# Column sums of the modulation vectors: one-column matmuls replaced by two wide matmuls and diagonal sums on VectorE

## The chip, the core and the metric

The kernel runs on one core of a Trainium2 chip. The number that counts is the device time of one execution in microseconds (us); where a time is given for a kernel it is the median of its runs. The engines are TensorE (PE; PEld is its weight load), VectorE (DVE), ScalarE (ACT), GpSimd (POOL) and SyncE (SP), which here issues the DMAs. TensorE writes to PSUM, and the other memory on the chip is SBUF.

## The reference, cut to what matters

Four layers work on x of shape (1024, 1024). Layer i uses mixer i mod 3: gated linear attention (GLA), spatial gating (SGU), forgetting attention (FoX), then GLA again. Each layer is modulated by a vector that depends only on the small input c:

```python
cond = jax.nn.silu(c)
for i in range(DEPTH):
    mod = (cond @ w_mod[i] + b_mod[i])[:, None, :]
    shift, scale, gate = jnp.split(mod, 3, axis=-1)
    h = rms_norm(x, norm_pre_g[i]) * (1.0 + scale) + shift
    ...  # the mixer turns h into o
    x = x + gate * rms_norm(o, norm_post_g[i])
```

The change concerns how `shift` and `scale` of layers 1, 2 and 3 are brought into the form in which they are used.

## The kernel before

All of the input and output projections run on TensorE in three passes (lines 357 to 359): a weight and an activation are each split into a rounded part (float32r, the type of the fast multiplication, names `whi`, `wo`, `hTh`) and the rest (`wlo`, `hTl`), and three of the four products are summed in a PSUM tile `pj`. There are three PSUM tiles for the projections (tag `pj`), three for small work (`pm`) and two for scores (`pb`).

The modulation is 3072 numbers a layer, in six pieces of 512 (`j` = 0 to 5 in `mod_pieces`). For a piece, an accumulator `acc` of 128 x 512 (a tile of tag `md`, of which there are four) starts as zero with the bias in row 0. For each of eight blocks of 128 rows of `w_mod`, VectorE adds the block times a column of `cond` (L264). The piece is then the sum of `acc` over its 128 partitions, and `finish` takes this sum:

- Pieces 4 and 5 (the gate) are wanted as rows, the same in each partition. ScalarE rounds `acc` to `hi` (L289), GpSimd takes the rest `lo` (L290), and TensorE multiplies both with a square of ones (`onesr`, L291 and L292).
- Pieces 0 to 3 (shift and scale) are wanted as columns, the feature in the partition, as `SH` and `G` of 128 x 8. TensorE takes each 128 x 128 block of `acc` as the weights against one column of ones (L274), four matmuls with one output column each. These are full float32, and each is two matmul records in the trace. VectorE copies the four columns to `SH` (L278) or combines them into `G` (L281).

Layer 0 takes its pieces in a wide form at the start (`wide=True`, PSUM tile `pb`). For the later layers the pieces are background work: while layer l runs, the pieces 0 to 3 of layer l+1 are worked on, one step of a piece at a time, so that 12 of these `finish` calls fall into layers 0, 1 and 2, four in each (names in the trace: `pm<-ones,md`).

The order in which each engine does its instructions is not the order of the Python text. The compiler front end that builds the program orders the instructions of each engine by a simulated timeline, and each engine then does its own list strictly in order. Work tiles of tag `s2` (shown as `s`) come from a pool of 28.

In the GLA layer `mix` builds 7 levels of decayed products on VectorE and ScalarE (lines 702 to 712), whose scores TensorE takes (L723) and VectorE merges into `cmix` (L725); a running state `st` is updated at L778. In the FoX layer `weigh` takes scores (L1119, L1120), and VectorE adds a bias and takes the maximum in one instruction with an accumulator (L1123, L1128, shown as a custom operation and the read of its accumulator); `do_v` brings projections from `pj` to `v` (L1025 on ScalarE, L1026 on VectorE).

Of the kernel before, what the change touches and what calls it, by code (L numbers as in the profile page):

```python
# [8 lines left out]
F32 = mybir.dt.float32  # L9
F32R = mybir.dt.float32r  # L10
U8 = mybir.dt.uint8
AF = mybir.ActivationFunctionType
ALU = mybir.AluOpType
AX = mybir.AxisListType

P = 128
# [78 lines left out]
class Trunk:  # L95
# [124 lines left out]
        nc.gpsimd.memset(self.cmix, 0.0)  # L220


    def mod_pieces(self, l, cols, wide=False):
        nc, a = self.nc, self.a
        if cols[0] < 4 and self.G[l] is None:
            self.G[l] = self.cp.tile([P, KT], F32, name=f"G{l}")
            self.SH[l] = self.cp.tile([P, KT], F32, name=f"SH{l}")
        if cols[-1] >= 4:
            self.gg[l] = self.cp.tile([P, D], F32, tag="gg", name=f"gg{l}", bufs=2)
        G, SH, gg = self.G[l], self.SH[l], self.gg[l]  # L230
        pieces, ends = [], []

        def col(j):
            st = {}

            def begin():
                acc = self.sp.tile([P, 512], F32, tag="md", name=self.nm("md"), bufs=4)
                nc.gpsimd.memset(acc, 0.0)
                nc.sync.dma_start(out=acc[0:1, :], in_=a["b_mod"][l:l + 1, j * 512:(j + 1) * 512])
                st["acc"] = acc  # L240
                if wide:
                    st["pt"] = self.ps("pb")
                    nc.tensor.matmul(st["pt"][:, 0:4], self.ident, self.zero, start=True, stop=False)

            def step(kp):
                w = []
                if wide:
                    wt = self.wp.tile([P, 2, 512], F32, tag="whl", name=self.nm("md2"))
                    self.last["sp"] = nc.sync.dma_start(out=wt, in_=a["w_mod"][l, 2 * kp * P:(2 * kp + 2) * P, j * 512:(j + 1) * 512]
                                      .rearrange("(i p) n -> p i n", p=P))  # L250
                    w = [wt[:, i, :] for i in range(2)]
                else:
                    for i in range(2):
                        w.append(self.sp.tile([P, 512], F32, tag="md", name=self.nm("md"), bufs=4))
                for i in range(2):
                    kt = 2 * kp + i
                    if wide and kp % 2 and i:
                        for c in range(4):
                            nc.tensor.matmul(st["pt"][:, c:c + 1], w[i][:, c * P:(c + 1) * P], self.cond[:, kt:kt + 1],
                                             start=False, stop=False)  # L260
                        continue
                    if not wide:
                        nc.sync.dma_start(out=w[i], in_=a["w_mod"][l, kt * P:(kt + 1) * P, j * 512:(j + 1) * 512])
                    ins = nc.vector.scalar_tensor_tensor(st["acc"], w[i], self.cond[:, kt:kt + 1], st["acc"],  # L264
                                                         op0=ALU.mult, op1=ALU.add)
                    if not wide:
                        self.tc.keep_in_program_order(ins)

            def finish():
                acc = st["acc"]  # L270
                if j < 4:
                    pt = st["pt"] if wide else self.ps("pm")
                    for i in range(4):
                        self.last["tensor"] = nc.tensor.matmul(pt[:, i:i + 1], acc[:, i * P:(i + 1) * P], self.ones[:, 0:1],  # L274
                                                               start=not wide, stop=not wide or i == 3)
                    k0 = (j % 2) * 4
                    if j < 2:
                        nc.vector.tensor_copy(SH[:, k0:k0 + 4], pt[:, 0:4])  # L278
                    else:
                        g0 = self.vcol["gpre"] + l * KT + k0  # L280
                        nc.vector.scalar_tensor_tensor(G[:, k0:k0 + 4], pt[:, 0:4], 1.0, self.vec[:, g0:g0 + 4],  # L281
                                                       op0=ALU.add, op1=ALU.mult)
                else:
                    cs = (j - 4) * 512
                    gp = self.s2([512])
                    nc.sync.dma_start(out=gp, in_=a["norm_post_g"][l:l + 1, cs:cs + 512].partition_broadcast(P))
                    pt = self.ps("pm")
                    hi, lo = self.s2([512], F32R), self.s2([512], F32R)
                    nc.scalar.copy(hi, acc)  # L289
                    nc.gpsimd.tensor_tensor(lo, acc, hi.bitcast(F32), op=ALU.subtract)  # L290
                    nc.tensor.matmul(pt, self.onesr, hi, start=True, stop=False)  # L291
                    nc.tensor.matmul(pt, self.onesr, lo, start=False, stop=True)  # L292
                    nc.vector.tensor_tensor(gg[:, cs:cs + 512], pt, gp, op=ALU.mult)

            pieces.append(lambda: (begin(), step(0)))
            if ends:
                pieces.append(ends.pop())
            for kp in range(1, 4):
                pieces.append((lambda kp: lambda: step(kp))(kp))
            ends.append(finish)  # L300
            if wide or j == cols[-1]:
                pieces.append(ends.pop())

        for j in cols:
            col(j)
        return pieces
# [1026 lines left out]
```

## Time and profile before

| | |
|---|---|
| runs | 2140.03, 2142.40, 2142.49 us; median 2142.4 us |
| profiled execution | 2135.41 us |
| its span from first to last instruction | 2133.7 us |
| TensorE clock granted, mean | 0.994 |
| TensorE busy | 2070.1 us, 97% of the span |
| VectorE busy | 1304.2 us, 61% |
| ScalarE busy | 906.4 us, 42% |
| GpSimd busy | 802.2 us, 38% |

Outside its span the profiled execution has 1.7 us, and it took 7.0 us less than the median of the runs. Layer 0 runs to about 560 us, layer 1 to about 850 us, layer 2 to about 1600 us, and the rest is layer 3. A matmul's duration in the trace overlaps the next one's, so what a matmul costs is read from one start to the next.

### The profile page before, as it was taken

What the parts mean: (1) busy time and instruction counts of PE and PEld (TensorE: products, weight loads), DVE (VectorE), ACT (ScalarE), POOL (GpSimd) and SP (SyncE); (2) the same over time, 40 slices, a digit from 0 to 9 for tenths busy, and PEclk for the clock granted to TensorE, in tenths of its full rate; (3) what the DMA queues carried; (4) which work ended last, traced back from release to release, by engine and by line L of the source; (5) the groups of instructions that cost most, each with busy time, mean ns of one, the idle gap of its engine ahead of it and who ended that gap; (6) DMA issues with size and microseconds to landing.
All of it is one profiled execution on the core that took longest, in us unless ns stands there. A gap on an engine that the chain in (4) does not pass through costs nothing. (4 is left out here: it accounts for less than half of the span.)

```text
span 2133.7 us, 35726 instructions
## 1 busy us (share of the span) xinstructions
PE 2070.1 (97%) x13637; PEld 1848.4 (87%) x13637; DVE 1304.2 (61%) x2884; ACT 906.4 (42%) x1905; POOL 802.2 (38%) x735
## 2 busy tenths in 40 slices
PE   6999999999999999999999999999999999999998
PEld 6888998988998888898788898898678899899987
DVE  7686878645465425556656656656865654776642
ACT  4555333335322114544445445445545655343331
POOL 5433333355343332535333333333323441342351
PEclk9999999999999999999999999999999999999999
DMA  8132222424425432423223323323424320112322
GB/s 295 41 90 79 84 81 96 149 99 138 138 76 164 132 117 99 136 71 104 81 75 100 90 70 101 88 71 100 148 81 143 101 60 21 50 46 69 127 90 95
DMA packets 160339, 213.09 MB, mean 100 GB/s; under 512 B 13906, under 2 KB 96402, under 8 KB 160170
## 3 DMA queue, kind: packets, MB, share of 16 engines
q1 hardware_dynamic: 160170, 210.82, 31.5%
q8 instruction: 107, 1.75, 0.4%
q14 instruction: 62, 0.51, 0.1%
HBM read 172.44 MB, written 29.95 MB: 95 GB/s over the span
## 5 line engine op out<-in xcount | busy, mean ns | idle before, releaser
L357 PE MATMUL pj<-whi,hTh 128*128 128x256 f32 (+1 forms) x2048 | 598.6, 292 | 3.4 <-ACT s L1040 2.7
L359 PE MATMUL pj<-whi,hTl 128*128 128x256 f32 (+1 forms) x2048 | 591.7, 289 | 1.9 <-DVE hTl L459 1.9
L358 PE MATMUL pj<-wlo,hTh 128*128 128x256 f32 (+1 forms) x2048 | 591.4, 289 | 0.0
L357 PEld LDWEIGHTS pj<-whi,hTh 128*128 128x128 f32 x2048 | 393.9, 192 | 10.2 <-issue 3.1
L359 PEld LDWEIGHTS pj<-whi,hTl 128*128 128x128 f32 x2048 | 393.4, 192 | 6.2 <-DVE hTl L459 2.3
L358 PEld LDWEIGHTS pj<-wlo,hTh 128*128 128x128 f32 x2048 | 393.7, 192 | 5.0 <-issue 2.2
L322 POOL TENSOR_TENSOR wlo<-wraw,whi 128x1024 fp32r<-128x1024 f32 (+2 forms) x112 | 266.1, 2385 | 299.8 <-ACT whi L321 287.9
L357 PE MATMUL pj<-hTh,whi 128*128 128x512 f32 x640 | 255.3, 399 | 0.0
L359 PE MATMUL pj<-hTh,wlo 128*128 128x512 f32 x640 | 254.6, 398 | 0.0
L358 PE MATMUL pj<-hTl,whi 128*128 128x512 f32 x640 | 253.1, 395 | 0.0
L264 DVE SCALAR_TENSOR_TENSOR md<-md,cond,md 128x512 f32<-128x512 f32 x184 | 171.4, 933 | 38.6 <-DMA md<-in_w_mod 36.5
L1113 POOL TENSOR_TENSOR db<-s,mneg 128x128 f32<-128x128 f32 x128 | 67.9, 538 | 268.8 <-DVE mx L1128 157.4
L321 ACT CAST whi<-wraw 128x1024 fp32r<-128x1024 f32 (+2 forms) x112 | 110.8, 991 | 95.7 <-PE pj L358 74.6
L359 PEld LDWEIGHTS pj<-hTh,wlo 128*128 128x128 f32 x640 | 121.0, 189 | 24.8 <-issue 0.9
L357 PEld LDWEIGHTS pj<-hTh,whi 128*128 128x128 f32 x640 | 121.2, 189 | 23.8 <-issue 0.7
L358 PEld LDWEIGHTS pj<-hTl,whi 128*128 128x128 f32 x640 | 120.9, 189 | 23.8 <-issue 0.7
L1147 ACT COPY s<-pm 128x512 f32<-128x512 f32 (+2 forms) x192 | 87.5, 480 | 124.9 <-PE pm L1145 122.8
L1134 ACT ACTIVATE p<-p,ng 128x256 f32<-128x256 f32 (+7 forms) x128 | 99.5, 778 | 81.1 <-DVE ng L1132 80.1
L357 PE MATMUL pj<-wo,hTh 128*128 128x512 f32 x320 | 126.3, 396 | 1.2 <-ACT s L489 1.2
L358 PE MATMUL pj<-wo,hTh 128*128 128x512 f32 x320 | 125.2, 391 | 0.0
L359 PE MATMUL pj<-wo,hTl 128*128 128x512 f32 x320 | 123.5, 392 | 0.0
L1123 DVE CUSTOM_DVE_ANT_0 p<-pb,s 128x512 f32<-128x512 f32 (+3 forms) x160 | 82.3, 526 | 60.8 <-PE pb L1120 58.7
(219 smaller groups left out, 4030.5 us busy)
## 6 DMA issues: line engine op xcount, KB each, us to landing
md<-in_w_mod SPq DMA_DIRECT2D x160, 256.0 KB
wraw<-in_gla_w_in SPq DMA_DIRECT2D x32, 512.0 KB
yd<-s SPq DMA_DIRECT2D x50, 256.0 KB
xd<-x SPq DMA_DIRECT2D x24, 512.0 KB
wraw<-in_sgu_w_in SPq DMA_DIRECT2D x24, 512.0 KB
x<-xd SPq DMA_DIRECT2D x24, 512.0 KB
wraw<-in_fox_w_in SPq DMA_DIRECT2D x48, 256.0 KB
s<-yd SPq DMA_DIRECT2D x42, 256.0 KB
```

The costliest lines, as they stand in the source:

```text
L264: ins = nc.vector.scalar_tensor_tensor(st["acc"], w[i], self.cond[:, kt:kt + 1], st["acc"], op0=ALU.mult, op1=ALU.add)
L321: nc.scalar.copy(hi, raw)
L322: nc.gpsimd.tensor_tensor(lo, raw, hi.bitcast(F32), op=ALU.subtract)
L357: nc.tensor.matmul(ps, lh, rh, start=first, stop=False)
L358: nc.tensor.matmul(ps, lh, rl, start=False, stop=False)
L359: nc.tensor.matmul(ps, ll, rh, start=False, stop=last)
L1113: nc.gpsimd.tensor_tensor(db, nf[p, ib // 4, hb][:, qc], mneg, op=ALU.add)
L1123: nc.vector.tensor_tensor_reduce(e[:, c * 512:c * 512 + d0], sp[:, 0:d0], nf[p, c, hb][:, 0:d0], op0=ALU.add, op1=ALU.max, scale=1.0, scal ...
L1134: nc.scalar.activation(e[:, 0:n + P], e[:, 0:n + P], AF.Exp, bias=ng, accum_out=ls[:, 0:1])
L1147: nc.scalar.copy(et[:, 0:nb * P], pt[:, 0:nb * P])
```

## The change

A function `row_sums` is made from what pieces 4 and 5 did, with the engine of the subtraction as a parameter. Pieces 0 to 3 of layers 1 to 3 now call it too, with the subtraction on VectorE. The PSUM tile then holds the 512 sums in each of its 128 partitions. Column i is taken out by VectorE: block i times the identity, summed along the row, goes to one column of `SH` or `G` (a multiplication with an accumulator, written for each of the four blocks). For `G` one more small instruction follows. Layer 0 and pieces 4 and 5 compute as before.

```diff
+    def row_sums(self, acc, sub):
+        nc = self.nc
+        pt = self.ps("pm")
+        hi, lo = self.s2([512], F32R), self.s2([512], F32R)
+        nc.scalar.copy(hi, acc)
+        sub.tensor_tensor(lo, acc, hi.bitcast(F32), op=ALU.subtract)
+        nc.tensor.matmul(pt, self.onesr, hi, start=True, stop=False)
+        nc.tensor.matmul(pt, self.onesr, lo, start=False, stop=True)
+        return pt
...
                 if j < 4:
-                    pt = st["pt"] if wide else self.ps("pm")
-                    for i in range(4):
-                        self.last["tensor"] = nc.tensor.matmul(pt[:, i:i + 1], acc[:, i * P:(i + 1) * P], self.ones[:, 0:1],
-                                                               start=not wide, stop=not wide or i == 3)
                     k0 = (j % 2) * 4
-                    if j < 2:
-                        nc.vector.tensor_copy(SH[:, k0:k0 + 4], pt[:, 0:4])
...
                     else:
+
+                        pt = self.row_sums(acc, nc.vector)
+                        col = (SH if j < 2 else G)[:, k0:k0 + 4]
+                        dg = self.s2([4, P])
+                        for i in range(4):
+                            nc.vector.tensor_tensor_reduce(dg[:, i, :], pt[:, i * P:(i + 1) * P], self.ident, op0=ALU.mult,
+                                                           op1=ALU.add, scale=1.0, scalar=0.0, accum_out=col[:, i:i + 1])
+                    if j < 2 and wide:
+                        nc.vector.tensor_copy(SH[:, k0:k0 + 4], col)
+                    elif j >= 2:
                         g0 = self.vcol["gpre"] + l * KT + k0
-                        nc.vector.scalar_tensor_tensor(G[:, k0:k0 + 4], pt[:, 0:4], 1.0, self.vec[:, g0:g0 + 4],
+                        nc.vector.scalar_tensor_tensor(G[:, k0:k0 + 4], col, 1.0, self.vec[:, g0:g0 + 4],
                                                        op0=ALU.add, op1=ALU.mult)
...
-                    pt = self.ps("pm")
-                    hi, lo = self.s2([512], F32R), self.s2([512], F32R)
-                    nc.scalar.copy(hi, acc)
-                    nc.gpsimd.tensor_tensor(lo, acc, hi.bitcast(F32), op=ALU.subtract)
-                    nc.tensor.matmul(pt, self.onesr, hi, start=True, stop=False)
-                    nc.tensor.matmul(pt, self.onesr, lo, start=False, stop=True)
+                    pt = self.row_sums(acc, nc.gpsimd)
```

The order of the instructions changes with it. The first place is TensorE in layer 1, at the first column piece for layer 2 (`pm_6792` before, `pm_6818` after). Before:

```order
L359 MATMUL pj_6866<-hTh,wlo_6642 128x512
L357 MATMUL pj_6866<-hTh,whi_6641 128x512
L274 MATMUL pm_6792<-ones,md_6592 128x1 x4
L358 MATMUL pj_6866<-hTl,whi_6641 128x512
L359 MATMUL pj_6866<-hTh,wlo_6642 128x512
```

After (line numbers in the changed file are higher by 16 here; L229 and L230 are the two wide matmuls of `row_sums`):

```order
L373 MATMUL pj_6898<-hTh,whi_6667 128x512
L229 MATMUL pm_6818<-s_1063_6819,onesr 128x512
L374 MATMUL pj_6898<-hTl,whi_6667 128x512
L375 MATMUL pj_6898<-hTh,wlo_6668 128x512
L373 MATMUL pj_6898<-hTh,whi_6673 128x512
L230 MATMUL pm_6818<-s_1064_6820,onesr 128x512
L374 MATMUL pj_6898<-hTl,whi_6673 128x512
```

Four one-column matmuls at one spot have become two of 512 columns, with three projection matmuls between them.

The second place is VectorE in layer 0, at the first column piece for layer 1 (`SH_139`), between two units of `mix`. Before:

```order
L725 COPY_PREDICATED cmix<-lmask,pb_2742 128x256
L708 TENSOR_TENSOR s_428_2746<-s_428_2746,qk_1987 128x64x4
L712 TENSOR_TENSOR s_428_2746<-s_428_2746,qk_1987 128x2x32x4
L278 COPY SH_139<-pm_2637 128x4
L702 TENSOR_TENSOR s_433_2789<-s_278_1772 128x2x64x2
L705 TENSOR_TENSOR s_433_2789<-s_278_1772 128x128x2
```

After (the subtraction, L228, stands six rows ahead of the first row here; `ISA` is the multiplication with its sum, and then the read of the accumulator, and two such pairs of the four are left out):

```order
L794 SCALAR_TENSOR_TENSOR st_2555<-st_2546,ebl_2244,pm_2553 128x256
L794 SCALAR_TENSOR_TENSOR st_2593<-st_2555,ebl_2244,pm_2591 128x256
L296 ISA s_413_2644,SH_139<-pm_2637,ident 128x128
L296 ISA SH_139 128x1
...
L296 ISA s_413_2644,SH_139<-pm_2637,ident 128x128
L296 ISA SH_139 128x1
L718 TENSOR_TENSOR s_417_2652<-s_278_1772 128x2x2x64
L721 TENSOR_TENSOR s_417_2652<-s_278_1772 128x4x64
```

One small copy in the middle of the unit's levels has become eight instructions ahead of the first level of that unit.

The third place is VectorE in the FoX layer, at the first column piece for layer 3, where three tiles of `v` are taken from `pj`. Before:

```order
L264 SCALAR_TENSOR_TENSOR md_12200<-md_12204,cond,md_12200 128x512
L1026 COPY s_2138_12230<-pj_12231 128x128
L1026 COPY s_2138_12230<-pj_12306 128x128
L278 COPY SH_8576<-pm_12209 128x4
L1026 COPY s_2138_12230<-pj_12361 128x128
```

After, from the same accumulation step on (L1144 is the maximum of the scores, before at L1128; the repeated pairs are left out):

```order
L275 SCALAR_TENSOR_TENSOR md_12252<-md_12256,cond,md_12252 128x512
L228 TENSOR_TENSOR s_2156_12263<-md_11343,s_2155_12262 128x512
L1144 ISA p_12391,mx_12392<-pb_12395,db_12393 128x128
...
L1148 TENSOR_REDUCE ng_12399<-mx_12392 128x1
L296 ISA s_2157_12268,SH_8628<-pm_12261,ident 128x128
...
L1148 TENSOR_REDUCE ng_12454<-mx_12447 128x1
L1151 RECIPROCAL ls_12331<-ls_12331 128x1
L1042 COPY s_2165_12288<-pj_12289 128x128
L1042 COPY s_2165_12288<-pj_12364 128x128
L1042 COPY s_2165_12288<-pj_12419 128x128
```

The three copies out of `pj` have moved behind the subtraction, two units of scores and the four sums.

## Rows read from the trace of the kernel before

**Rows 1.** The page's busy times and instruction counts of each engine.

```profile
PE 2070.1 (97%) x13637; PEld 1848.4 (87%) x13637; DVE 1304.2 (61%) x2884; ACT 906.4 (42%) x1905; POOL 802.2 (38%) x735
```

**Rows 2.** Busy time by stretch: length, PE, PEld, DVE, ACT, POOL, clock, DMA.

```profile
275.00:560.00 285.00, 281.05 (x1857) 257.42 (x1856) 176.92 (x328) 116.09 (x263) 113.28 (x105) 1.00 0.34 111
560.00:850.00 290.00, 290.00 (x1604) 253.53 (x1603) 141.72 (x179) 69.56 (x114) 104.41 (x70) 1.00 0.38 123
...
1130.00:1450.00 320.00, 318.32 (x2501) 281.58 (x2500) 202.89 (x643) 153.84 (x336) 117.03 (x120) 1.00 0.30 85
...
325.00:350.00 25.00, 24.89 (x177) 23.41 (x176) 23.01 (x47) 10.44 (x26) 10.00 (x8) 1.00 0.28 85
350.00:375.00 25.00, 22.61 (x174) 21.84 (x172) 20.97 (x38) 9.77 (x26) 8.82 (x7) 1.00 0.29 83
```

**Rows 3.** Waits of PE in 275 to 560 us: total, times, longest.

```profile
PE pm L782 <- DVE st L778: 3.1, 2, 2.4
```

**Rows 4.** Timeline of PE in layer 1 around one column piece: start, duration.

```profile
681.96 0.39 PE L357 MATMUL pj<-hTh,whi 128*128 128x512 f32 x1
682.19 0.95 PE L274 MATMUL pm<-ones,md 128*128 128x1 f32 x8
683.00 0.49 PE L358 MATMUL pj<-hTl,whi 128*128 128x512 f32 x1
683.32 0.40 PE L359 MATMUL pj<-hTh,wlo 128*128 128x512 f32 x1
683.55 0.40 PE L357 MATMUL pj<-hTh,whi 128*128 128x512 f32 x1
```

**Rows 5.** Timeline of PE in layer 1 at a gate piece, adjoining wide matmuls.

```profile
621.63 0.39 PE L291 MATMUL pm<-s,onesr 128*128 128x512 f32 x1
621.86 0.40 PE L292 MATMUL pm<-s,onesr 128*128 128x512 f32 x1
622.10 0.39 PE L357 MATMUL pj<-hTh,whi 128*128 128x512 f32 x1
```

**Rows 6.** Groups by line: count, busy, mean ns, idle before and its releasers.

```profile
L274 PE MATMUL pm<-ones,md 128*128 128x1 f32 x96 | 11.4, 240 | 0.0
L289 ACT CAST s<-md 128x512 fp32r<-128x512 f32 x8 | 5.0, 620 | 13.1 <-DVE md L264 11.1 <-DVE ng L1132 2.0
L292 PE MATMUL pm<-s,onesr 128*128 128x512 f32 x8 | 3.9, 483 | 0.6 <-POOL s L290 0.6
L291 PE MATMUL pm<-s,onesr 128*128 128x512 f32 x8 | 3.6, 446 | 0.3 <-ACT s L289 0.2
L290 POOL TENSOR_TENSOR s<-md,s 128x512 fp32r<-128x512 f32 x8 | 11.0, 1374 | 21.3 <-ACT s L289 21.2
L570 DVE TENSOR_TENSOR hTl<-s,hTh 128x512 fp32r<-128x512 f32 x32 | 28.1, 918 | 11.6 <-ACT hTh L569 11.4
```

**Rows 7.** Timeline of DVE in layer 2: copies out of pj, then two maxima.

```profile
1370.92 0.47 DVE L1026 COPY s<-pj 128x128 f32<-128x128 f32 x2
1371.32 0.14 DVE L281 SCALAR_TENSOR_TENSOR G<-pm,vec 128x4 f32<-128x4 f32 x1
1371.39 0.27 DVE L1026 COPY s<-pj 128x128 f32<-128x128 f32 x1
1371.59 0.27 DVE L1128 CUSTOM_DVE_ANT_0 p<-pb,db 128x128 f32<-128x128 f32 x1
1371.79 0.07 DVE L1128 DVE_READ_ACCUMULATOR2_ANT mx<- 128x1 f32 x1
1371.79 0.28 DVE L1128 CUSTOM_DVE_ANT_0 p<-pb,db 128x128 f32<-128x128 f32 x1
```

**Rows 8.** Timeline of PE in layer 2 behind those copies, with idle time.

```profile
1371.25 0.39 PE L357 MATMUL pj<-whi,hTh 128*128 128x256 f32 x1 [0.56 <-DVE s L1026]
```

**Rows 9.** The subtraction L570 on DVE: ns min/median/max.

```profile
L570 DVE TENSOR_TENSOR hTl<-s,hTh x32: 674/686/2487, 804.1 to 1615.0; 128x512 fp32r<-128x512 f32 x32
```

**Rows 10.** Waits of SP's DMA queue, total, times, longest.

```profile
SPq L263 <- PE pm L274: 22.7, 7, 8.3
```

More of the change, by code (lines that the diff above doesn't have):

```diff
@@ L271, in finish @@
                 if j < 4:
-                    pt = st["pt"] if wide else self.ps("pm")
-                    for i in range(4):
-                        self.last["tensor"] = nc.tensor.matmul(pt[:, i:i + 1], acc[:, i * P:(i + 1) * P], self.ones[:, 0:1],
-                                                               start=not wide, stop=not wide or i == 3)
                     k0 = (j % 2) * 4
-                    if j < 2:
-                        nc.vector.tensor_copy(SH[:, k0:k0 + 4], pt[:, 0:4])
-                    else:
+                    if wide:
+                        pt = st["pt"]
+                        for i in range(4):
+                            self.last["tensor"] = nc.tensor.matmul(pt[:, i:i + 1], acc[:, i * P:(i + 1) * P],
+                                                                   self.ones[:, 0:1], start=False, stop=i == 3)
+                        col = pt[:, 0:4]
+                    else:
+                        pt = self.row_sums(acc, nc.vector)
+                        col = (SH if j < 2 else G)[:, k0:k0 + 4]
+                        dg = self.s2([4, P])
+                        for i in range(4):
+                            nc.vector.tensor_tensor_reduce(dg[:, i, :], pt[:, i * P:(i + 1) * P], self.ident, op0=ALU.mult,
[3 more added lines that the diff above has]
+                    elif j >= 2:
                         g0 = self.vcol["gpre"] + l * KT + k0
-                        nc.vector.scalar_tensor_tensor(G[:, k0:k0 + 4], pt[:, 0:4], 1.0, self.vec[:, g0:g0 + 4],
+                        nc.vector.scalar_tensor_tensor(G[:, k0:k0 + 4], col, 1.0, self.vec[:, g0:g0 + 4],
                                                        op0=ALU.add, op1=ALU.mult)
```

## The prediction

> **What bounds the kernel now.** I read the page's busy times first. TensorE is busy for 2070.1 of 2133.7 us, 97%, and VectorE comes next with 61% [rows 1]. So all idle time of TensorE in the span is 63.6 us, and everything the kernel can gain elsewhere than in TensorE's own work lies in that. Busy time of TensorE counts overlapping matmuls, so I went on to the stretches in which the 12 column pieces fall. In 560 to 850 us, layer 1, TensorE is busy for 290.00 of 290.00 us and VectorE for 141.72: there only TensorE's own work counts. In 275 to 560 us it is 281.05 of 285, in 1130 to 1450 us 318.32 of 320 [rows 2]. The reader is to see that each stretch is bound by TensorE, but not each with the same cover: in 325 to 350 us VectorE is busy for 23.01 of 25 us, and in the next 25 us TensorE has its largest gap, 2.4 us [rows 2], waiting for the state that VectorE updates [rows 3]. In that part of the GLA layer VectorE is nearly a second bound.
>
> **TensorE, the part removed.** A column piece is 4 matmuls, 8 records of one column each, with 8 loads of 128 columns of weights. The mean duration of 240 ns [rows 6] says little, since they overlap. I read from start to start: from the projection matmul at 681.96 to the third after it, at 683.55, it is 1.59 us with the piece between [rows 4]. Without the piece these are three steps of 0.23 us, the step between wide matmuls as 621.63, 621.86 and 622.10 show [rows 5], so 0.69 us. The piece costs 1.59 - 0.69 = 0.90 us. There are 96 records of this kind, which is 12 pieces, so 12 x 0.90 = 10.8 us.
>
> **TensorE, the part added.** Two wide matmuls with `onesr`. The same pair exists for the gate pieces: it begins at 621.63 and the next projection at 622.10, 0.47 us [rows 5]; 12 x 0.47 = 5.6 us. TensorE's own work falls by 10.8 - 5.6 = 5.2 us. A pair in a worse place, as part of a sequence of full float32 matmuls, has no such clean row; the mean durations of the pair, 446 and 483 ns, are longer than the 390 to 400 here [rows 5, 6], by some 0.05 and 0.09 us. If all of that were a longer step, the pair would cost 0.61 us and the saving would be 3.5 us. I take 5.2, since in layer 1 the neighbours are those of the row, and a step, not a duration, counts.
>
> **The new latency.** Before, the matmuls needed `acc` alone. Now `hi` needs a ScalarE cast, 0.62 us, and `lo` a subtraction behind it. Both wide matmuls stand at fixed places in TensorE's list, so a late operand stops everything behind it, the projections above all. The nearest rows are the gate pieces, which take the same way: eight pairs waited 0.3 us for `hi` and 0.6 us for `lo` in total, 0.9 us or 0.11 us a piece, although there GpSimd needed 1374 ns for the subtraction [rows 6]. For 12 pieces that is 1.3 us. Below, the wait can be nothing. Above, the subtraction on VectorE has a row of its own kind, L570: median 686, mean 918, largest 2487 ns [rows 9]. If each of the 12 were the largest, and all of the excess over the median ended on TensorE, it would be 12 x 1.8 = 21.6 us. I take 1.3 us, by the gate pieces, since they are the same helper, and with a mean subtraction that is 0.46 us shorter.
>
> **VectorE.** A sum with its accumulator read takes one step of 0.20 us for 128 x 128, from 1371.59 to 1371.79 [rows 7], so 0.8 us for four, and with a subtraction at the mean 0.92 us [rows 6] each piece adds 1.7 us. The `SH` copies go, some 0.07 us each [rows 7]. That is 12 x 1.7 = 20 us more on an engine with 829 us idle. What hides it is TensorE's projection work, and in layer 1 that cover is whole. In the GLA part four pieces add 6.8 us to a nearly full engine; uncovered they would cost 6.8 us. The four sums also wait for `lo`'s matmul at the head of VectorE's list, and in the new order the first level of the next unit of `mix` stands behind them. In the new order those scores are also later in TensorE's list, so I take nothing here, and keep 6.8 us as the upper end.
>
> In layer 2 three copies out of `pj` now stand behind the subtraction, two units of scores and the four sums. By rows this is about 0.7 + 2 x 0.3 + 0.8 us and a scaling with some small reductions, about 3 us. TensorE has three `pj` tiles, and at the same kind of place it already waited 0.56 us for such a copy [rows 8]. There are two of these places, where a column piece falls beside `do_v`, so from nothing to 6 us; I take nothing extra, since TensorE's list has moved the scores ahead too, and let the range hold it.
>
> **Others.** ScalarE gets 12 x 0.62 = 7.4 us at 42% busy, covered by the projections. Each new pair keeps its `pm` tile until VectorE has summed, so two of three remain for transposes for some 2 us; that is part of the same cover. The accumulator's `md` tile was freed by the one-column matmuls, and SP's loads of `w_mod` waited 22.7 us for that [rows 10]. Now the subtraction frees it, about one cast and one subtraction behind the last addition, sooner or later by less than 2 us, and it is four tiles of background work. No DMA is added.
>
> **The sum.** For the profiled execution: 2135.4 - 5.2 + 1.3 = 2131.5 us. It ran 7.0 us below the median of the runs, 2142.4, so the forecast for a median is 2142.4 - 3.9 = 2138.5 us. A measurement of this kernel can tell about 0.2%, 4.3 us: the forecast lies just inside, and its own range, 2136 to 2141 us, on both sides of that bound.
>
> **Rivals.**
>
> *The saving whole, and old gaps closed.* The order changes in the GLA part on four engines, so the gaps of 3.1 us on the state [rows 3] can go, and no operand is late: 2142.4 - 5.2 - 3.1 = 2134.1 us. For it: VectorE's new list puts the state updates together, ahead of the sums. Against it: it is luck, and the sums hold VectorE where it is fullest.
>
> *VectorE the second bound in the GLA layer.* The four pieces there come on the path at their full 6.8 us: 2142.4 - 5.2 + 6.8 = 2144.0 us, no change that can be told. For it speak 23.01 of 25 us [rows 2], against it that TensorE waited only 3.1 us for the state in all of 275 to 560 us [rows 3].
>
> *The subtraction held up by GpSimd, slower.* L570 and the new subtraction have the same shape and both inputs in SBUF. Its largest duration is 3.6 times the median [rows 9]. If in the eight pieces of layers 0 and 2 it takes 1.8 us more, and TensorE stands at `lo` for that time, it is 8 x 1.8 = 14.4 us, and 2142.4 - 5.2 + 14.4 = 2151.6 us. It decides the sign from 5.2 us in total on, and is slower by 0.2% from 9.5 us, 1.2 us in each of the eight. For it: the mean is 232 ns over the median, so some are held long. Against it: a mean excess of 0.23 us in 12 pieces is only 2.8 us, and in layer 1 TensorE has three projection matmuls between the two wide ones. The Trainium skill, SBUF — State Buffer, Who interferes with whom, states that a VectorE instruction with two SBUF inputs contends with a GpSimd instruction that reads SBUF, and that one blocks the other for a whole instruction. By that rule, the durations of L570 would look as they do, and moving the subtraction onto VectorE would bring TensorE under GpSimd's long subtractions; the sums, with one input in PSUM, would stay free.
>
> *The change does not do what it says*, where the pair costs TensorE as much as the eight records: the row of 0.47 us speaks against it; the time would be 2142.4 + 1.3 = 2143.7 us.
>
> **How the numbers follow.** Chances: the forecast 0.46, the saving whole 0.19, VectorE bound 0.14, held up by GpSimd 0.18, no saving 0.03. The forecast's half below 2138.1 us counts as faster, so faster 0.19 + 0.22 = 0.41; same 0.24 + 0.12 + 0.03 = 0.39; slower 0.18 and 0.02 of the VectorE case, 0.20. The range goes from 2133, a little below the saving whole, to 2147, which holds the VectorE case with the `pj` copies late and leaves out most of the case with GpSimd.
>
> **What would show it.** In the profile of the changed kernel the step from the projection before a column piece to the one behind it in layer 1 should be 0.44 us shorter than 1.59, the wide pair should be there 20 times instead of 8, TensorE's waits at L229 and L230 should sum to 1 to 3 us over 20 pairs, VectorE's busy time should rise by about 20 us, and layer 1's stretch should shrink by about 1.7 us. The prediction would be wrong if TensorE waits at L230 for several us, if L228's mean is far over 0.92 us, if TensorE's waits for `cmix`, `st` or the `pj` copies grow by over 5 us, or if the new order moves gaps elsewhere in layers 0 and 2.

## The result, and the profile after

The changed kernel takes 2153.0 us in the median of 6 runs (2150.63 to 2160.82), beside 2142.4 us for the kernel before: a ratio of 1.0057 [1.0044, 1.0070]. It is slower by 10.6 us, where 3.9 us of gain were forecast, and outside the range given. On another chip the same pair gave 2153.09 us and 1.0048 [1.0032, 1.0065]. The profiled execution of after is the slowest of its runs, 2160.82 us; the second profile, of a run of 2152.00 us, is shown beside it where a sum depends on that.

The page's first part, to set beside [rows 1]:

```profile
PE 2076.3 (96%) x13565; PEld 1850.9 (86%) x13565; DVE 1327.5 (61%) x2986; ACT 911.3 (42%) x1917; POOL 797.0 (37%) x735
```

TensorE has 72 matmul records fewer, and yet it is busy for 6.2 us longer. VectorE has 23.3 us more, about the 20 us of the forecast. The stretches of [rows 2], in the same columns:

```profile
275.00:560.00 285.00, 280.24 (x1821) 255.97 (x1820) 186.88 (x381) 121.99 (x274) 115.51 (x107) 0.99 0.34 111
560.00:850.00 290.00, 290.00 (x1597) 253.43 (x1596) 147.31 (x212) 71.60 (x118) 102.16 (x69) 1.00 0.39 123
...
1130.00:1450.00 320.00, 310.17 (x2423) 274.40 (x2422) 204.44 (x648) 150.77 (x334) 111.31 (x118) 0.99 0.29 84
```

In the GLA layer TensorE's idle time grows by 0.8 us (285 less 280.24, before 285 less 281.05), in layer 1 there is none, and in the FoX layer it grows from 1.7 to 9.8 us in this stretch alone. To get whole layers I cut the span at the last multiplication with the gate of each layer (L488, in the changed file L504); by these cuts the layers of the kernel before end at 529, 911 and 1671 us, and the 560, 850 and 1600 us given ahead of the prediction are rough. Layers 1 and 2 of the kernel before:

```profile
529.28:911.07 381.79, 381.01 (x2156) 334.64 (x2155) 192.68 (x266) 117.07 (x219) 144.42 (x118) 1.00 0.38 125
911.07:1671.01 759.94, 740.83 (x5437) 646.62 (x5435) 479.96 (x1399) 373.52 (x806) 284.89 (x295) 1.00 0.32 96
```

The same of the kernel after, first profile:

```profile
531.84:912.70 380.86, 380.08 (x2140) 333.51 (x2139) 199.41 (x299) 118.92 (x223) 141.47 (x118) 1.00 0.39 125
912.70:1694.27 781.57, 748.30 (x5406) 651.30 (x5404) 493.81 (x1432) 373.75 (x809) 283.34 (x294) 0.98 0.31 94
```

And in its second profile:

```profile
530.01:910.07 380.06, 379.26 (x2133) 332.70 (x2132) 198.31 (x299) 119.15 (x223) 142.60 (x118) 1.00 0.39 125
910.07:1688.58 778.51, 746.85 (x5412) 650.47 (x5411) 493.84 (x1432) 374.71 (x809) 283.50 (x294) 0.98 0.32 94
```

Layer 1 is shorter by 0.9 and 1.7 us. The FoX layer is longer by 21.6 and 18.6 us, where the profiled executions differ from that of before by 25.4 and 16.6 us: the loss lies in this layer (the profile of before ran 7.0 us below its median, so part of this difference is luck; in the first experiment below, where only the FoX layer has its old pieces, it is 762.6 us long). The 21.6 us are two things. TensorE's idle time in the layer, length less busy, goes from 19.1 to 33.3 us, 14.2 more. Its busy time rises by 7.5 us with less work in it, and the granted clock, 0.98 instead of 1.00, says why: some matmuls ran at half clock.

How time is lost is seen at the third column piece of the layer, the place of [rows 7, 8]. Timeline of after, engines TensorE, ScalarE and VectorE together:

```profile
1373.28 0.28 PE L375 MATMUL pj<-whi,hTl 128*128 128x256 f32 x1
...
1374.26 0.97 ACT L1163 COPY s<-pm 128x512 f32<-128x512 f32 x2
...
1375.11 0.63 ACT L227 CAST s<-md 128x512 fp32r<-128x512 f32 x1
...
1375.34 0.69 DVE L1139 CUSTOM_DVE_ANT_0 p<-pb,s 128x512 f32<-128x512 f32 x1
...
1376.14 0.30 PE L1135 MATMUL pb<-s,s 128*128 128x128 f32 x1 [1.79 <-ACT s L227]
...
1378.23 0.68 DVE L228 TENSOR_TENSOR s<-md,s 128x512 fp32r<-128x512 f32 x1
...
1378.97 0.72 PE L230 MATMUL pm<-s,onesr 128*128 128x512 f32 x1 [1.20 <-DVE s L228]
...
1379.23 1.15 ACT L1150 ACTIVATE p<-p,ng 128x1024 f32<-128x1024 f32 x1 [3.49 <-DVE ng L1148]
...
1379.73 0.29 DVE L296 CUSTOM_DVE_ANT_0 s<-pm,ident 128x128 f32<-128x128 f32 x1
...
1381.14 0.57 ACT L1041 COPY s<-pj 128x128 f32<-128x128 f32 x3
1381.44 0.22 DVE L1151 RECIPROCAL ls<-ls 128x1 f32<-128x1 f32 x2
1381.58 0.47 DVE L1042 COPY s<-pj 128x128 f32<-128x128 f32 x2
...
1381.90 0.58 PE L373 MATMUL pj<-whi,hTh 128*128 128x256 f32 x1 [0.43 <-DVE s L1042]
```

The last projection that has a `pj` tile starts at 1373.28. All three tiles are then full, and the copies out of them (L1041, L1042) start only at 1381.14, 7.9 us later. Before, the same copies came 0.65 us behind the projection:

```profile
1368.30 0.36 PE L359 MATMUL pj<-whi,hTl 128*128 128x256 f32 x1
...
1368.95 0.61 ACT L1025 COPY s<-pj 128x128 f32<-128x128 f32 x3
```

In the 8 us of after TensorE has scores, transposes and the two wide matmuls, and waits between them, here 1.79 and 1.20 us. For the first the profile names the cast, which had ended 0.40 us before; the maximum of an earlier score (L1139), which frees a score tile, ended at 1376.03, and is the likelier releaser. VectorE is busy for 4.94 us of the 5 ahead of 1379.07 (the windows at the end of this text): it is the engine that scores and piece wait for.

This place is not all of the loss. Stretches cut at about the same work before and after take 2.3 us more around the first piece (1195 to 1235 us before, 1197 to 1239.3 after), 7.1 us more around the second and third (1285 to 1400, 1289.3 to 1411.4), 3.6 us more around the fourth, which has no `do_v` behind it (1440 to 1500, 1451.4 to 1515), and 7.4 us more in the stretch behind the last piece. That stretch before, and then after:

```profile
1500.00:1560.00 60.00, 54.89 (x376) 41.63 (x375) 48.16 (x155) 36.44 (x77) 16.72 (x21) 1.00 0.41 124
...
1515.00:1582.40 67.40, 59.03 (x370) 44.90 (x369) 50.29 (x158) 36.84 (x77) 16.63 (x21) 0.90 0.35 110
```

### The profile page after: what moved, and what is told of

The parts are those of the page before. It is cut to its first block, busy times and chain, and to the rows that moved or that the text cites. A ratio compares the mean times of both kernels' runs of the same rounds, so it can differ in the third digit from the quotient of the medians.

```text
span 2158.9 us, 35682 instructions
## 1 busy us (share of the span) xinstructions
PE 2076.3 (96%) x13565; PEld 1850.9 (86%) x13565; DVE 1327.5 (61%) x2986; ACT 911.3 (42%) x1917; POOL 797.0 (37%) x735
## 5 line engine op out<-in xcount | busy, mean ns | idle before, releaser
L338 POOL TENSOR_TENSOR wlo<-wraw,whi 128x1024 fp32r<-128x1024 f32 (+2 forms) x112 | 263.0, 2356 | 313.7 <-ACT whi L337 301.2
L1150 ACT ACTIVATE p<-p,ng 128x256 f32<-128x256 f32 (+7 forms) x128 | 99.6, 778 | 108.7 <-DVE ng L1148 107.5
L428 POOL TENSOR_TENSOR r<-r,neghalf 128x1 f32<-128x1 f32 (+2 forms) x104 | 113.9, 1101 | 7.0
```

Of the source, the lines that this page charges most:

```text
L338: nc.gpsimd.tensor_tensor(lo, raw, hi.bitcast(F32), op=ALU.subtract)
L428: nc.gpsimd.tensor_tensor(r, r, self.half[:, 0:1].to_broadcast([P, n]) if n > 8 else self.half[:, 0:n], op=ALU.pow)
L1150: nc.scalar.activation(e[:, 0:n + P], e[:, 0:n + P], AF.Exp, bias=ng, accum_out=ls[:, 0:1])
```

## The experiments

First come two tables of what was measured. The first has each kernel with the median of the kernel before on the same chip, its ratio, the length of its FoX layer, and the time from the start of the last projection to the first copy out of `pj`, at the first and the third column piece of that layer, where `do_v` follows (read from timelines as above). Length and lateness are those of one profile each. The medians are of 11 or 12 runs, but of 6 for the change, 5 for `one early tile` and 4 for `old, late tile`; one of the 12 runs of the shifted change took 6965 us, and without it its median is 2144.2 us.

| kernel | us, before | ratio | FoX layer, us | copies late by, us |
|---|---|---|---|---|
| before | | | 759.9 | 1.0, 0.7 |
| after | 2153.0, 2142.4 | 1.0057 [1.0044, 1.0070] | 781.6 | 5.4, 7.9 |
| after, again | 2153.1, 2144.1 | 1.0048 [1.0032, 1.0065] | 778.5 | 5.4, 7.9 |
| FoX with old pieces | 2139.5, 2141.7 | 0.9985 [0.9975, 0.9994] | 762.6 | 1.0, 0.7 |
| no `s2` tile | 2139.2, 2141.7 | 0.9990 [0.9981, 0.9999] | 765.8 | 1.0, 1.0 |
| old, three tiles | 2141.1, 2141.7 | 0.9994 [0.9983, 1.0005] | 763.8 | 1.1, 1.1 |
| old, VectorE load | 2144.7, 2141.7 | 1.0009 [0.9999, 1.0018] | 761.4 | 1.0, 0.7 |

The second has the runs that came after a theory was formed:

| kernel | us, before | ratio | FoX layer, us | copies late by, us |
|---|---|---|---|---|
| one late tile | 2147.3, 2143.0 | 1.0016 [1.0004, 1.0028] | 774.2 | 5.4, 5.6 |
| one early tile | 2136.5, 2143.0 | 0.9965 [0.9953, 0.9977] | 761.6 | 1.5, 1.5 |
| change, touched early | 2141.0, 2143.0 | 0.9988 [0.9979, 0.9997] | 763.9 | 1.6, 1.6 |
| change, shifted | 2144.4, 2143.0 | 1.0003 [0.9993, 1.0013] | 768.1 | 1.0, 1.5 |
| old, late tile | 2162.4, 2144.1 | 1.0086 [1.0073, 1.0099] | 777.8 | 6.0, 5.9 |
| old, early tile | 2148.0, 2144.1 | 1.0014 [1.0003, 1.0025] | 763.1 | 1.1, 1.1 |
| old, shifted | 2140.5, 2144.1 | 0.9984 [0.9972, 0.9995] | 764.8 | 1.0, 0.7 |

**Which layer, and which part.** Four kernels. In the first the pieces for layer 3, which fall into the FoX layer, go back to the one-column form, and layers 0 and 1 keep the change:

```diff
-                    if wide:
-                        pt = st["pt"]
+                    old = wide or l == 3
+                    if old:
+                        pt = st["pt"] if wide else self.ps("pm")
...
```

> The pieces of layer 3, which fall into the FoX layer, take the one-column matmuls again; those of layers 1 and 2 stay new. The two traces are level (+0.7 us) up to 850 us and differ by 22 us at the end of layer 2, so by every theory nearly all of the loss is in the FoX layer: 2140 to 2144 us, and layer 2's stretch as before. If the loss sat in layers 0 and 1 too: 2148 us or more.

2139.5 us, a little under the range: the loss is in the FoX layer alone, and the rest of the change gains. In the second all of the change's work stays, but none of its tiles is an `s2` tile:

```diff
-                        pt = self.row_sums(acc, nc.vector)
+                        hi = self.sp.tile([P, 512], F32R, tag="md", name=self.nm("md"), bufs=4)
+                        lo = self.sp.tile([P, 512], F32R, tag="md", name=self.nm("md"), bufs=4)
...
-                        dg = self.s2([4, P])
+                        dg = hi.rearrange("p (i t) -> p i t", t=P)
```

> The change with all its work, but the rounded part and the rest live in two tiles of the small pool of four that the modulation weights use, and the masked blocks go into the tile of the rounded part, so that no tile of the pool of 28 is taken. Theory 1: the FoX loss goes, 2137 to 2142 us. Theories 2 and 3: 2149 to 2155 us, as the change.

The loss is gone, with the cast, the subtraction, both wide matmuls and the sums in place. The third is the kernel before with three `s2` tiles for each column piece, of which four columns each are written and read:

```diff
+                        hi, lo, dg = self.s2([512]), self.s2([512]), self.s2([512])
+                        nc.scalar.copy(hi[:, 0:4], acc[:, 0:4])
+                        nc.vector.tensor_tensor(lo[:, 0:4], acc[:, 0:4], hi[:, 0:4], op=ALU.subtract)
...
+                        nc.vector.scalar_tensor_tensor(dg[:, 0:4], hi[:, 0:4], 0.0, col, op0=ALU.mult, op1=ALU.add)
...
```

> The kernel before, but each of the 12 pieces takes three more work tiles of the pool of 28 and holds them until its column is written, with a few 4-column instructions on them; the sums are still the one-column matmuls. Theory 1 (the three tiles take slots from the v tiles at the change of heads, so the copies out of pj and the projections behind them are late): 2148 to 2155 us, with the v copies behind the piece on VectorE. Theory 2 (the added VectorE work) and theory 3 (TensorE stands at the two wide matmuls, whose operands are late): 2142 to 2144 us.

No loss: that three more tiles are asked for is not enough. The fourth is the kernel before with the change's VectorE work as a load without a use, behind the matmuls:

```diff
+                    if not wide:
+                        nc.vector.tensor_tensor(acc, acc, acc, op=ALU.subtract)
+                        sm = self.small([4], tag="ss4")
+                        for i in range(4):
+                            nc.vector.tensor_tensor_reduce(self.junk[:, 0:P], self.ident, self.ident, op0=ALU.mult,
+                                                           op1=ALU.add, scale=1.0, scalar=0.0, accum_out=sm[:, i:i + 1])
```

> The kernel before, with VectorE work added behind each of the 12 pieces' matmuls: a subtraction of 512 columns in place and four 128 x 128 products with sums into a spare tile, 1.5 us or more a piece, no new tile of the pool of 28 and nobody waiting for it but the column's copy. Theory 2: 2148 us or more, with most of it in the FoX layer. Theories 1 and 3: 2142 to 2145 us.

2 us by the ratio and 3 us by the medians, at most 4 by the interval, and the FoX layer, 761.4 us, is no longer than in the other kernels without the loss. So neither the added operations nor the number of tiles makes the loss by itself; tiles and the long chain together do. What is left is the order in which the tiles are had. The list of ScalarE in the built program at the first piece of the FoX layer, with the engine that each instruction waits for, before and after:

```
L1025 COPY s_2137_12229<-pj_12231 128x128 [waits Pool_49]
```

```
L227 CAST s_2155_12262<-md_11343 128x512 [waits Pool_49]
L1150 ACTIVATE p_12316,ls_12331<-p_12316,ng_12329 128x1024 [waits DVE_49]
L1041 COPY s_2164_12287<-pj_12289 128x128
```

The wait for GpSimd, which stood at the first copy to `v`, has gone to the cast to `hi`; the copy behind it waits for no one, it stands later in the list. From that comes the queue theory: `s2` tiles are handed out in the order of the program text. `finish` stands directly ahead of `do_v`, so the tiles of `v` come behind `hi`, `lo` and `dg`, and `dg` is taken only when the first sum can write it, behind both wide matmuls.

**One tile, late or early.** Both kernels have all of the change's work and one `s2` tile. In the first it is `dg` (`hi` and `lo` as in the kernel without `s2` tiles), written for the first time behind the wide matmuls:

```diff
-                        dg = hi.rearrange("p (i t) -> p i t", t=P)
+                        dg = self.s2([4, P])
```

> The new pieces with the rounded part and the rest in tiles of md, as in the run without s2 tiles (2139.2 us), and only the masked blocks in an s2 tile, which is first written behind both wide matmuls. Queue theory (s2 tiles are handed out in the order of the program text, so the tiles of v, asked for behind this one, are not to be had before the sums begin; the copies out of pj and with them the projections stop): the loss comes back whole with this one tile, 2148 to 2155 us, and TensorE stands at the first and third column piece of the FoX layer. Pressure theory (three tiles held for long): one tile of three, at most a third of the 11 us, 2139 to 2143 us. Cost of the added operations: as without s2 tiles, 2139 us.

In the second it is `hi`, written first of all; `lo` lies in `md`, and `dg` in the tile of `hi`.

> The new pieces with only the rounded part in an s2 tile, which is written first of all; the rest goes to a tile of md and the masked blocks into the tile of the rounded part, which is so held from the cast to the sums. Queue theory: v stands behind the cast alone, 2138 to 2142 us. Pressure theory: one tile held over the whole chain, a third of the loss, 2143 us, the same as with one late tile.

The two differ by 10.8 us, on one chip. They differ in more than the place of the first write, since the first kernel takes two `md` tiles a piece and the second one. The kernel without `s2` tiles differs from the first in `dg` alone: between these two the late tile costs 0.26% by the ratios (1.0016 and 0.9990, on two chips), some 5.6 us, and 8.4 us of FoX layer. The rest of the 10.8 us may belong to the `md` tile; that was not tried. Their FoX layers, the late tile:

```profile
912.88:1687.06 774.18, 747.60 (x5401) 651.10 (x5401) 489.01 (x1432) 375.88 (x810) 284.22 (x295) 0.98 0.32 95
```

and the early tile:

```profile
910.54:1672.18 761.64, 737.58 (x5404) 644.74 (x5402) 485.25 (x1432) 375.45 (x810) 281.89 (x295) 0.99 0.32 96
```

The late tile lost a little less than expected, the early one lost nothing and is the fastest kernel of all, where the pressure theory had them alike. The timeline at the third piece, late tile:

```profile
1375.85 0.28 PE L381 MATMUL pj<-whi,hTl 128*128 128x256 f32 x1
...
1377.40 0.62 ACT L295 CAST md<-md 128x512 fp32r<-128x512 f32 x1 [0.42 <-DVE md L275]
...
1381.40 0.58 ACT L1047 COPY s<-pj 128x128 f32<-128x128 f32 x3
```

and early tile:

```profile
1367.46 0.28 PE L381 MATMUL pj<-whi,hTl 128*128 128x256 f32 x1
...
1368.48 0.62 ACT L295 CAST s<-md 128x512 fp32r<-128x512 f32 x1
...
1369.00 0.44 ACT L1047 COPY s<-pj 128x128 f32<-128x128 f32 x2
```

**The change, with one small write ahead.** All three tiles stay, and are held longer:

```diff
+                        dg = self.s2([4, P])
+                        nc.scalar.copy(dg[:, 0, 0:4], acc[:, 0:4])
                         pt = self.row_sums(acc, nc.vector)
...
-                        dg = self.s2([4, P])
```

> The change whole, with its three s2 tiles, but the tile for the masked blocks is asked for first and four columns of it are written by a small ScalarE copy ahead of the cast. It is held longer than in the change. Queue theory: the tiles of v now stand only behind the subtraction, and most of the loss goes: 2139 to 2145 us. Pressure theory: three tiles are held as long or longer, so the loss stays: 2149 to 2155 us. Late operands at the wide matmuls as the cause: nothing about them is changed, 2149 to 2155 us.

2141.0 us, against 2153. The copies to `v` now stand behind the subtraction and are late by 1.6 us.

**The kernel before, made slow.** No wide matmul and no sums: the old columns, a chain without a use in an `md` tile `m`, and one `s2` tile that takes the columns behind it (its value is the columns plus zero).

```diff
...
+                        nc.scalar.copy(m, acc)
+                        nc.vector.tensor_tensor(m, acc, m, op=ALU.subtract)
+                        nc.scalar.copy(m, m)
+                        nc.vector.tensor_tensor(m, m, m, op=ALU.add)
+                        tl = self.s2([512])
+                        nc.vector.scalar_tensor_tensor(tl[:, 0:4], m[:, 0:4], 0.0, col, op0=ALU.mult, op1=ALU.add)
+                        col = tl[:, 0:4]
...
```

> The kernel before with its one-column matmuls, and for each column piece a chain with no use: a ScalarE copy, a VectorE subtraction, a second ScalarE copy and a VectorE addition in a tile of md, and behind it one s2 tile that is written for the first time. No wide matmul, no sums. Queue theory: v stands behind that tile, so the loss appears in the kernel before: 2147 to 2153 us, TensorE late at the first and third piece of the FoX layer. Late operands at the wide matmuls as the cause: there are none, 2141 to 2146 us by the added work alone.

Its control asks for `tl` ahead of the chain and writes four columns at once:

```diff
+                        tl = self.s2([512])
+                        nc.scalar.copy(tl[:, 4:8], acc[:, 0:4])
...
-                        tl = self.s2([512])
```

> As the run with the old columns, the chain and the late s2 tile, but four columns of that tile are written by a small ScalarE copy ahead of the chain. All the work and the time for which the tile is held stay or grow. Queue theory: 2141 to 2146 us, what the added work costs by itself. Pressure theory and cost of the added work: the same time as with the late tile.

2162.4 and 2148.0 us: 14.4 us for the place at which one tile is asked for and first written, more than the 6 us or so between the two expectations. Both are dearer than expected; the chain itself costs, in layer 1 too (387.0 and 384.6 us for that layer, before 381.8), where the two are only 2.4 us apart. In the FoX layer they are 14.7 us apart. At the third piece, late tile:

```profile
1383.23 0.28 PE L369 MATMUL pj<-whi,hTl 128*128 128x256 f32 x1
...
1389.16 0.58 ACT L1035 COPY s<-pj 128x128 f32<-128x128 f32 x3
```

and early tile:

```profile
1373.77 0.28 PE L370 MATMUL pj<-whi,hTl 128*128 128x256 f32 x1
...
1374.79 0.20 ACT L280 COPY s<-md 128x4 f32<-128x4 f32 x1
1374.89 0.44 ACT L1036 COPY s<-pj 128x128 f32<-128x128 f32 x2
```

**The place moved.** One line in the FoX layer brings each later background step one place later, so that the first and third `finish` stand behind `do_v`:

```diff
+        self.bg.insert(0, lambda: None)
         units = [(p, ib, hb) for p in range(NP) for ib in range(NT) for hb in range(2)]
```

In the change, and in the kernel before:

> The change whole, with one empty step put in front of the background steps of the FoX layer, so that all later ones come one place later: the first and third column piece then finish behind the projection of v instead of directly ahead of it. Queue theory: no v tile is asked for behind the masked blocks' tile, but tiles for the query and key of the next pair are, with one projection between; 2137 to 2144 us. Pressure theory: the same three tiles held as long in the same layer, 2147 to 2155 us. Late operands at the wide matmuls as the cause: 2147 to 2155 us.

> The kernel before with the empty step in front of the background steps of the FoX layer, as control for the change with that step (2144.4 us, where the change loses about half of what it lost). If the shift costs nothing by itself: 2140 to 2144 us, and the rest of the loss of the shifted change belongs to the change, tiles asked for behind the masked blocks at other places. If the shift itself costs: 2144 to 2148 us, and the shifted change has lost all of its own loss.

2144.4 and 2140.5 us. The copies to `v` are in time again (1.0 and 1.5 us), but the shifted change is 0.19% slower than the shifted kernel before by the two ratios (1.0003 / 0.9984), where the early tile is 0.35% faster than before. Of the 0.9% between the change and the early tile the shift gives back 0.4%; against the change touched early (0.9988), which has the same tiles as the shifted one, 0.3% of 0.6 to 0.7% are left. Other tiles now stand behind `dg`; that these make the rest was not tried, and stays open.

**The change once more.**

> The change as it is, beside the others on one chip. Every theory: 2150 to 2156 us. Queue theory: in the profile the FoX layer alone is longer, by 10 us or more, half of it idle time of TensorE and half stretches at the lower granted clock.

2153.1 us, as expected, and a FoX layer longer by 18.6 us. Of these 12.6 us are idle time of TensorE and 6.0 us busy time, so not half and half. Its rows are shown in the first section.

## Why the prediction was wrong

**The bound, and TensorE's saving: right.** 5.2 us were forecast. In layer 1 four pieces gave 0.9 and 1.7 us, forecast 1.7. The early-tile kernel, where no gap hides it, has 2064.2 us of TensorE busy time, 5.9 less than [rows 1]. The forecast of 2138.5 us is 0.9982 of the kernel before; the three kernels that keep all of the change's work and lose the late tile have 0.9965, 0.9988 and 0.9990. The pair costs what [rows 5] said, from one start to the next 0.23 us a matmul, in layer 1 of after:

```profile
685.17 0.40 PE L373 MATMUL pj<-hTh,whi 128*128 128x512 f32 x1
685.40 0.40 PE L229 MATMUL pm<-s,onesr 128*128 128x512 f32 x1
685.63 0.39 PE L374 MATMUL pj<-hTl,whi 128*128 128x512 f32 x1
...
686.32 0.40 PE L230 MATMUL pm<-s,onesr 128*128 128x512 f32 x1
686.55 0.39 PE L374 MATMUL pj<-hTl,whi 128*128 128x512 f32 x1
```

**The operands' latency: right in size, in part by luck.** Groups by line, as in [rows 6]:

```profile
L228 DVE TENSOR_TENSOR s<-md,s 128x512 fp32r<-128x512 f32 x12 | 11.0, 920 | 6.7 <-ACT s L227 6.6
L229 PE MATMUL pm<-s,onesr 128*128 128x512 f32 x20 | 9.4, 471 | 0.3 <-ACT s L227 0.2
L230 PE MATMUL pm<-s,onesr 128*128 128x512 f32 x20 | 9.1, 456 | 1.9 <-DVE s L228 1.2 <-POOL s L228 0.6
```

The mean subtraction is 920 ns (taken: 918), and TensorE waited 2.2 us at 20 pairs, where eight waited 0.9: the 1.3 us of the sum. But it did not come as 0.11 us a piece: nearly all of the growth is the one wait of 1.20 us at the third piece of the FoX layer, shown above, and in the second profile, where that wait is 0.32 us, the total is 1.6 us.

**VectorE in the GLA layer: nearly right.** The layer is longer by 2.6 us in the first profile and 0.7 us in the second, of at most 6.8; with the early tile it is 0.2 us (529.5). None of this can be told from noise: the kernel before with the shift, whose instructions in this layer are the same, has 533.6 us here, 4.4 us more than before.

**The copies out of `pj`: the step that failed.** The prediction saw them move behind the subtraction, the scores and the sums, took "about 3 us" a place from VectorE's rows, "from nothing to 6 us" in all, and then "nothing extra", since TensorE's list had moved the scores ahead. They came 4.4 and 7.2 us later than before. The reason for the move was not asked for. It was not VectorE's work alone that set their place but the tile they write, which is to be had only behind `dg`: ScalarE's half of the same copies, for which the prediction had no term, went back in its list as well, behind a softmax (L1150) for whose maximum ScalarE stood idle for 3.49 us. The moved scores were no cover either. They need the maxima that VectorE takes, and VectorE had the cast's subtraction, two accumulation steps and the softmax in that same stretch. So the sign that the prediction had named, longer waits for the `pj` copies, is not to be seen: TensorE waits at the scores instead. Its waits in the FoX layer (total, times, longest), before, and then after:

```profile
PE pb L1119 <- DVE mx L1123: 2.5, 2, 1.8
PE pj L357 <- DVE s L1026: 0.6, 1, 0.6
...
PE pb L1135 <- DVE mx L1139: 4.3, 5, 1.3
PE pj L373 <- DVE s L1042: 0.4, 1, 0.4
```

The early-against-late pairs show this cause. The term that was put at nothing measures 13 to 15 us: 0.6 to 0.7% between the change (1.0057, 1.0048) and the change touched early (0.9988), with 781.6 and 778.5 us of FoX layer against 763.9. The lateness of the copies, 4.4 + 7.2 us, is near to this but is not the same thing: the work around the first piece took only 2.3 us longer, and time was also lost around the fourth piece and behind it, which the prediction did not look at. The experiments show that the late first write makes the loss; which tiles carry it to the places without `do_v` stays open.

**What no term had.** Part of the loss is the clock of TensorE behind such gaps (last section). Rival three, "held up by GpSimd", gave 2151.6 us, near to the 2153.0 measured, by a mechanism that did not occur: TensorE waited 1.2 us for this subtraction at L230 in all, not 14.4, and at the longest of these waits the subtraction itself took 0.68 us (L228 at 1378.23, above). Single subtractions are long, 1974 ns at most:

```profile
L228 DVE TENSOR_TENSOR s<-md,s x12: 678/686/1974, 261.6 to 1469.1; 128x512 fp32r<-128x512 f32 x12
```

The Trainium skill, SBUF — State Buffer, Who interferes with whom, has a VectorE instruction with two SBUF inputs contend with a GpSimd instruction that reads SBUF. The trace agrees as far as durations go: the two longest, 1951 and 1974 ns, start at 722.06 and 744.20 us, both while a GpSimd subtraction (L338) of 2.4 us runs, and end 0.5 us behind it. Both lie in layer 1 and not in layers 0 and 2, where the rival had them, and TensorE waited for neither. A number that comes out near is no evidence for its mechanism.

## What to carry to other kernels

Where tiles of a pool are handed out in the order of the program, a new tile's first write sets when all later tiles of that pool can be had: look which tile is asked for next, and who stands still without it. Take such a tile from a pool that the critical path doesn't use, reuse one that is already written, or write a few columns of it early; the change with one `s2` tile written first runs in 2136.5 us, 0.9965 [0.9953, 0.9977] of the kernel before, and beats both. When an order shows copies moving back, ask what they wait for before pricing the move with durations.

## What the runs showed of the hardware

TensorE's clock fell to half after gaps that are short by themselves. Windows of after with the granted clock in the third column from the right, each pair the 5 us ahead of a fall (only the width shown here) and the stretch behind it:

```profile
1374.07:1379.07 5.00, 2.01 (x16) 1.59 (x14) 4.94 (x15) 1.65 (x5) 0.90 (x1) 1.00 0.48 132
1379.07:1385.90 6.83, 6.13 (x25) 5.44 (x26) 3.42 (x25) 3.35 (x11) 0.87 (x2) 0.50 0.18 60
...
1537.91:1542.91 5.00, 2.37 (x19) 1.59 (x14) 4.18 (x12) 4.73 (x7) 0.45 (x1) 1.00 0.11 26
1542.91:1553.15 10.24, 9.05 (x44) 6.93 (x45) 6.58 (x18) 3.72 (x11) 2.32 (x3) 0.50 0.48 142
```

TensorE was busy for 2.01 and 2.37 of 5 us, and then ran at 1.2 GHz instead of 2.4 for 6.83 and 10.24 us, though it was busy for nearly all of that; ahead of the fall at 1471.23 us it was busy for 3.69 of 5. So a gap is paid twice. Over the FoX layer a mean clock of 0.98 in 781.57 us withholds 0.02 x 781.57, some 16 us, in this run, before under 4 us (1.00 in 759.94); TensorE's busy time in the layer, 7.5 us up with less work, shows how much of it was felt. The stretches at half clock in the FoX layer add up to 30.7 and 27.3 us in the two profiles of the change and to 30.7 us in both kernels with one late tile, to 13.7 to 13.9 us in the three with a tile written early, and to 6.9 us before. Falls between 1060 and 1520 us, where the pieces lie, are in all four of these profiles in which the copies are late by 5 us or more, and in none of the three with an early tile. But the second fall shown here is not the change's own: the old kernel with the early tile has one of 10.2 us at that place, the early tile one of 6.8 us, and so not all of the 7.4 us behind the last piece is owed to the late tile. The old kernel with the early tile there:

```profile
1500.00:1560.00 60.00, 53.94 (x357) 40.38 (x356) 45.62 (x150) 35.30 (x75) 18.61 (x24) 0.91 0.39 124
```

The Trainium skill, TensorE: Matmul & The Clock Gate, HAM oscillation — how this bites in real kernels, describes this: idle gaps inside a kernel bring the array back to half rate, and the work behind them pays. The trace agrees: ahead of the fall to 0.50 at 1379.07 us stand gaps of 1.79 and 1.20 us, here on VectorE's work. Which part of the loss would be left with the clock held up was not measured.
